# 2 KB pages for all buffers but the activations, one split for each product, and a new order of products in a Strassen short-convolution kernel

## The chip, the cores and the metric

The kernel runs on one core of one Trainium2 chip. The metric is the device time of one execution in microseconds. Before the change it is 792.23 us, the median of 3 runs (791.69 to 792.39).

## The reference

One layer of a gated short-convolution block, on one sequence of 1024 frames with 1024 channels, all in float32. `w_in` is 1024 x 8192 (four branches of 2048), `conv_w` is 3 x 2048, `w_out` is 2048 x 1024.

```python
u = rms_norm(h, pre_norm)
z, bg, cg, v = split(u @ w_in, 4)
y = bg * causal_dwconv(cg * v, conv_w) * silu(z)
m = y @ w_out
out = h + rms_norm(m, post_norm)
```

## The kernel before

**Arithmetic.** TensorE multiplies in `fp32r`. Every operand is split into a high part (the rounded value, ScalarE, line 140) and a low part (value minus high, VectorE, line 141), and a product is three matmuls: low x high, high x low, high x high (lines 189 to 191). On top of this stands one level of Strassen's method in the Winograd form: a product of 2 x 2 blocks takes seven block products, named a, b, c, e, d, f and g, instead of eight.

**Pairs.** The 2048 channels of a branch are taken in 16 chunks of 128. A chunk makes two *pairs* p: the even one multiplies the columns of cg and v, the odd one those of z and bg. A pair is seven products; a product is 4 x 3 = 12 matmuls of 512 columns. Pair 0 is done as plain products and pair 1 among the preparation; the loop of line 646 runs over p = 2 to 31 and takes the products of each in `ORDER`, "abcedfg".

**Weights of a pair.** `fetch` loads two row blocks of `w_in` into one tile `raw` of 8 KB per partition (two DMAs of 512 KB, line 121), one or two pairs ahead. `add_s` forms four sums of blocks on GpSimd (POOL): e, then c, d, f (lines 133 to 137), in one tile `sum` with a single buffer. `split_w` splits two blocks with one ScalarE and one VectorE instruction of 128 x 1024 (part 0: a and b; 1: c and e; 2: d and f) and g alone with 128 x 512 (part 3). The parts of pair q = p + 1 are issued after the products b, e, f and g of pair p, so the weights are split five to seven products before use.

**Results of a pair.** Four products pile up in the PSUM bank x (a, c, d, g), two in v (e, f), and b has its own, y. `snap` (line 197) copies x after a and after c, and v after e, to SBUF; the next product into that bank waits for the copy. VectorE adds b, d and f to these copies (lines 213, 218, 223). After g of an even pair VectorE multiplies into `gpad` (line 236) and `conv` (lines 573 to 580) runs: a scaled copy on ScalarE (line 575), then two VectorE instructions of 128 x 1024 (line 577) into a tile `cv`, which has two buffers. The odd pair multiplies the other factors into `cv` and stores it (`y_done`).

**Side work.** `fetch_t` and `add_t` form the block combinations of `w_out` for one chunk (four subtractions, on VectorE for even p, lines 275 to 278), for p = 4, 6, ... 16 and 17; `add_y` forms those of y (line 257, or lines 261 to 263). Both store their result in DRAM.

**Output stage.** After pair 31 the seven products of the output projection run over 28 *units* of four 128 x 512 blocks, loaded by `fetch_unit` (one DMA of 1 MB each) and split by `split_unit`; `combine` and `finish` normalise, add the residual and store.

**Order.** The schedule is manual: each engine runs its instructions in the order in which the code issues them, and so does the queue of SP, which issues nearly all DMAs. An instruction that waits holds back all that is behind it on its engine.

**Buffers.** `raw` has three tiles of 8 KB per partition and `sum` one; the split weights `wp` three of 8 KB and two of 4 KB; `snp` five of 2 KB; `tmp` holds `gpad`, `cv` and one more of 2 KB; `up` has seven of 16 KB for the activations, which are split once; PSUM has eight banks.

## Time and profile before

| | |
|---|---|
| median of the runs shown | 792.23 us |
| the profiled execution: its own time | 791.43 us |
| its span, first to last instruction | 789.6 us |
| TensorE (PE) busy | 781.3 us, 3494 matmuls |
| VectorE (DVE) busy | 532.2 us, 578 instructions |
| ScalarE (ACT) busy | 309.3 us, 425 instructions |
| GpSimd (POOL) busy | 293.4 us, 197 instructions |
| HBM read and written | 84.4 and 29.4 MB |

In the profile's rows L141 is line 141 of the kernel, and `w<-sum,w` means that tile w is written from tiles sum and w. A row of the timeline has the start and the duration in us, the engine, the line, the operation, the tiles and shapes, the count, and in brackets the idle time before it with what ended that. Times are from the start of the span. PEld is TensorE's weight load, SPq the DMA queue of SP. Two names are used below: T is the start of the first matmul behind product g of an even pair, and a *lo* (*hi*) is the VectorE (ScalarE) instruction of a split.

### The profile page before, as it was taken

The numbers are of one execution on the slowest core, as the hardware profiler recorded it, in microseconds if no ns is written. First come the engines' busy times: TensorE is split into PE (matmuls) and PEld (weight loads), VectorE is DVE, ScalarE is ACT, GpSimd is POOL, SyncE is SP. The second block draws the span as 40 slices with busy tenths as digits, with TensorE's granted clock in tenths as the row PEclk, the third lists the DMA queues.
The fourth block names the chain that finished last, engine by engine and source line by source line (L and its number), as shares of the span: only waits on it lengthen the run. The fifth ranks groups of instructions, "written<-read, shape, count | busy, mean of one in ns | idle before, by whom it ended". The sixth has DMA issues, their size and how long they took to land.

```text
span 789.6 us, 9038 instructions
## 1 busy us (share of the span) xinstructions
PE 781.3 (99%) x3494; PEld 647.9 (82%) x3494; DVE 532.2 (67%) x578; ACT 309.3 (39%) x425; POOL 293.4 (37%) x197
## 2 busy tenths in 40 slices
PE   9999999999999999999999999999999999999996
PEld 8888888888888888888888888888888888888885
DVE  6799676767676767586666666666666857633766
ACT  8555423333333333332333232333332636544441
POOL 2618644444444444456444444434443100000020
PEclk9999999999999999999999999999999999999999
DMA  9130370707061625246232414141505569455237
GB/s 319 56 99 8 94 238 16 253 1 253 26 228 43 212 67 187 93 164 207 95 127 75 147 54 148 53 148 52 180 22 198 215 233 415 180 198 213 107 110 263
DMA packets 94282, 114.38 MB, mean 145 GB/s; under 512 B 2920, under 2 KB 68512, under 8 KB 92192
## 3 DMA queue, kind: packets, MB, share of 16 engines
q1 hardware_dynamic: 94224, 113.81, 42.4%
q8 instruction: 27, 0.44, 0.2%
q14 instruction: 15, 0.12, 0.0%
q10 hardware_dynamic: 16, 0.00, 0.0%
HBM read 84.44 MB, written 29.36 MB: 144 GB/s over the span
## 4 chain that ended last, share of the span: by engine, by line
PE 98%; DVE 0%; DMA 0%; ACT 0%; issue 0%; DVEq 0%
PE px L189 14%; PE px L190 14%; PE px L191 14%; PE pv L189 7%; PE pv L191 7%; PE pv L190 7%; PE po_x L708 4%; PE po_x L709 4%; PE po_x L707 4%; PE py L189 4%; PE py L191 4%; PE py L190 4%; PE po_v L708 2%; PE po_v L709 2%; PE po_v L707 2%; PE pp L388 1%
## 5 line engine op out<-in xcount | busy, mean ns | idle before, releaser
L141 DVE TENSOR_TENSOR w<-sum,w 128x1024 fp32r<-128x1024 f32 x62 | 93.7, 1511 | 77.3 <-ACT w L140 77.3
L141 DVE TENSOR_TENSOR w<-raw,w 128x1024 fp32r<-128x1024 f32 (+1 forms) x62 | 98.3, 1587 | 5.2 <-ACT w L140 5.2
L140 ACT CAST w<-sum 128x1024 fp32r<-128x1024 f32 x62 | 65.0, 1049 | 63.1 <-issue 54.5
L577 DVE SCALAR_TENSOR_TENSOR cv<-gpad,cw,cv 128x1024 f32<-128x1024 f32 x32 | 63.7, 1989 | 20.2 <-ACT cv L575 19.6
L140 ACT CAST w<-raw 128x1024 fp32r<-128x1024 f32 (+1 forms) x62 | 51.5, 833 | 59.9 <-PE py L191 59.9
L228 POOL TENSOR_TENSOR gpad<-snc,sne 128x512 f32<-128x512 f32 x15 | 20.4, 1360 | 138.9 <-DVE snc L223 138.9
L136 POOL TENSOR_TENSOR sum<-raw 128x512 f32<-128x512 f32 x31 | 61.0, 1969 | 0.0
L220 POOL TENSOR_TENSOR sne<-sne,cv 128x512 f32<-128x512 f32 x15 | 20.4, 1363 | 100.6 <-DVE sne L218 85.2
L223 DVE TENSOR_TENSOR snc<-pv,snc 128x512 f32<-128x512 f32 x30 | 20.7, 691 | 54.3 <-PE pv L191 54.3
L747 POOL TENSOR_TENSOR acc<-acc,xr 128x512 f32<-128x512 f32 x4 | 6.9, 1719 | 133.1 <-DVE acc L746 133.1
L137 POOL TENSOR_TENSOR sum<-raw,sum 128x512 f32<-128x512 f32 x31 | 54.6, 1763 | 0.0
L133 POOL TENSOR_TENSOR sum<-raw 128x512 f32<-128x512 f32 x31 | 41.5, 1337 | 31.4 <-DVE w L141 31.4
L189 PE MATMUL py<-u_b,w 128*128 128x512 f32 x124 | 48.4, 391 | 0.0
L189 PE MATMUL px<-u_a,w 128*128 128x512 f32 x124 | 48.3, 390 | 0.0
L191 PE MATMUL py<-u_b,w 128*128 128x512 f32 x124 | 48.2, 389 | 0.0
L190 PE MATMUL py<-u_b,w 128*128 128x512 f32 x124 | 48.2, 389 | 0.0
L191 PE MATMUL px<-u_a,w 128*128 128x512 f32 x124 | 48.2, 389 | 0.0
L190 PE MATMUL px<-u_a,w 128*128 128x512 f32 x124 | 48.2, 389 | 0.0
L189 PE MATMUL px<-u_c,w 128*128 128x512 f32 x124 | 48.2, 389 | 0.0
L190 PE MATMUL px<-u_c,w 128*128 128x512 f32 x124 | 48.2, 389 | 0.0
L191 PE MATMUL px<-u_c,w 128*128 128x512 f32 x124 | 48.2, 389 | 0.0
L189 PE MATMUL pv<-u_e,w 128*128 128x512 f32 x124 | 48.2, 389 | 0.0
(259 smaller groups left out, 2073.7 us busy)
## 6 DMA issues: line engine op xcount, KB each, us to landing
raw<-in_sc_w_in SPq DMA_DIRECT2D x64, 512.0 KB, 5.4
y_d<-cv SPq DMA_DIRECT2D x16, 512.0 KB, 3.2
t<-in_sc_w_out SPq DMA_DIRECT2D x8, 1024.0 KB, 5.9
t_d<-t SPq DMA_DIRECT2D x8, 1024.0 KB, 4.3
s_d<-s SPq DMA_DIRECT2D x8, 768.0 KB, 3.6
s<-y_d SPq DMA_DIRECT2D x8, 512.0 KB, 4.5
xr<-in_x SPq DMA_DIRECT2D x8, 512.0 KB, 4.5
out<-acc SPq DMA_DIRECT2D x12, 256.0 KB, 2.5
```

Of the source, the lines that this page charges most:

```text
L133: nc.gpsimd.tensor_add(s[:, 1], a21, a22)
L136: nc.gpsimd.tensor_sub(s[:, 2], a11, a21)
L137: nc.gpsimd.tensor_sub(s[:, 3], a12, s[:, 0])
L140: nc.scalar.copy(hi, src)
L141: nc.vector.tensor_sub(lo, src, hi.bitcast(F32))
L189: nc.tensor.matmul(ps, lo, UH[i][:, k], start=first and k == 0, stop=False, skip_group_check=True)
L190: nc.tensor.matmul(ps, hi, UL[i][:, k], start=False, stop=False, skip_group_check=True)
L191: nc.tensor.matmul(ps, hi, UH[i][:, k], start=False, stop=last, skip_group_check=True)
L577: nc.vector.scalar_tensor_tensor(cv, gpad[:, j : j + L], tap(c, j), cv, op0=ALU.mult, op1=ALU.add)
L707: nc.tensor.matmul(ps, lo, u[:, 0, k], start=first, stop=False, skip_group_check=True)
L708: nc.tensor.matmul(ps, hi, u[:, 1, k], start=False, stop=False, skip_group_check=True)
L709: nc.tensor.matmul(ps, hi, u[:, 0, k], start=False, stop=last, skip_group_check=True)
```

## The change

All tiles but the activations, `gpad`, `cv` and a few of the ends become pages of 128 x 2 KB in one pool of 36. `fetch` fills four pages with four DMAs of 256 KB; each sum is a page (d overwrites a block of `raw`); each product's weights are two pages, split by one hi and one lo of 128 x 512. `cv` has one buffer. Products run in the order of `slots`: c e d f of pair p, then a and b of pair p + 1, then g of p. After product n, `prepare` issues the splits of all products whose nominal start (2.72 us each) lies less than 7 us behind that of product n + 1: of product n + 3, that is. The functions whose names begin with `deep` run only for chunks from `DEEP` on, and with `DEEP = 16` there are none; they are left out here.

```diff
+PAGES = 36
+DEEP = 16
+LEAD = 7.0
...
-    wp = ctx.enter_context(tc.tile_pool(name="wp", bufs=3))
-    raw = ctx.enter_context(tc.tile_pool(name="raw", bufs=3))
+    pages = ctx.enter_context(tc.tile_pool(name="pages", bufs=PAGES))
...
+    def page(name, dtype=F32, shape=(HB,)):
+        return pages.tile([P, *shape], dtype, tag="pg", name=name, bufs=PAGES)
...
     def fetch(p, rows=(0, 1)):
...
-            nc.sync.dma_start(raws[p][:, n], wiv[:, :, c0 : c0 + P])
+            for k in (0, 1):
+                if (p, n, k) not in raws:
+                    raws[p, n, k] = page(f"raw_{p}_{n}{k}", shape=(KH, P))
+                nc.sync.dma_start(raws[p, n, k], wiv[:, k * KH : (k + 1) * KH, c0 : c0 + P])
...
+    def add_s(p, kinds):
...
+        for i in kinds:
+            if i == "d":
+                t = block(p, 1, 0)
+                nc.gpsimd.tensor_sub(t, block(p, 0, 0), t)
+            else:
+                t = page(f"s{i}_{p}")
+                if i == "e":
+                    nc.gpsimd.tensor_add(t, block(p, 1, 0), block(p, 1, 1))
+                elif i == "c":
+                    nc.gpsimd.tensor_sub(t, sums[p, "e"], block(p, 0, 0))
+                else:
+                    nc.gpsimd.tensor_sub(t, block(p, 0, 1), sums[p, "c"])
+            sums[p, i] = t
...
+    def split_w(p, kinds):
...
+        for i in kinds:
+            hi, lo = (page(f"w{i}{h}_{p}", F32R) for h in "hl")
+            split(block(p, *BLOCK[i]) if i in BLOCK else sums[p, i], hi, lo)
+            wt[p, i] = hi, lo
...
     def add_t(j, eng):
...
+        for n in range(4):
+            nc.sync.dma_start(t_d[:, n, j], t[n])
...
     def square(t):
-        out = flat(raws[0][:, 0]) if t == 0 else junk
+        out = block(0, 0, 0).bitcast(BF16) if t == 0 else junk
...
-            fetch(2)
         rs = pre_rstd([t])
...
     low_plain(0, 1)
+    fetch(2)
...
-    split_w(2, 0)
+    split_w(2, "ab")
...
-    add_s(2, 0)
-    add_s(2, 1)
+    add_s(2, "ecdf")
     fetch(3)
     def conv(c):
-        cv = tmp.tile([P, L], F32, tag="cv", name=f"cv_{c}", bufs=2)
+        cv = tmp.tile([P, L], F32, tag="cv", name=f"cv_{c}")
...
-            split_w(2, 1)
+            split_w(2, "c")
             conv(0)
...
+    slots = [("a", 2), ("b", 2)]
+    for p in range(2, len(PAIRS)):
+        q = p + 1
...
+        for i in "cedf":
+            slots.append((i, p))
...
+        if q <= END:
+            slots.append(("a", q))
...
+                slots.append(("b", q))
+        slots.append(("g", p))
...
+    def prepare(n):
+        while ready[0] < len(slots) and at[ready[0]] < at[n + 1] + LEAD:
+            i, p = slots[ready[0]]
...
+            elif (p, i) not in wt:
+                split_w(p, i)
+            ready[0] += 1
...
+    for n, (i, p) in enumerate(slots):
...
+        product(p, i)
+        prepare(n)
+        after(p, i)
+        q, prev = p + 1, p // 2 - 1
...
+        if i == "c":
+            if p % 2 and p // 2 < DEEP:
+                nc.scalar.activation(sn[p, "a"], sn[p, "a"], AF.Silu)
+            if p in TODO:
+                fetch_t(TODO[p])
+            if p % 2 == 0 and p > 2:
+                fetch_s(prev)
...
+        elif i == "e":
+            add_s(q, "ec")
+        elif i == "d":
+            if p + 2 <= END:
+                fetch(p + 2)
+            add_s(q, "d")
+            if p % 2 == 0 and p > 2:
+                add_y(prev)
+        elif i == "f":
+            add_s(q, "f")
+            if p == 2:
+                add_y(0)
...
+        elif i == "g":
+            if p in TODO:
+                add_t(TODO[p], nc.gpsimd if p % 2 else nc.vector)
...
+        if p == END - 1 and i in "cd":
+            fetch_unit()
+        if p == END and i in "acdg":
+            split_unit()
+            fetch_unit()
```

The output stage follows: a unit is four pages with four DMAs of 256 KB and four splits of 128 x 512 (two of 128 x 1024 before), four units instead of five are split ahead of it, and the residual, the post-norm row and three of the result blocks become pages of 128 x 512 with a DMA each.

## The prediction

> **What bounds the kernel now.** I read the totals first, then the stretches, then TensorE's own waits.

> ```profile
> span 789.6 us, 9038 instructions
> ...
> PE 781.3 (99%) x3494; PEld 647.9 (82%) x3494; DVE 532.2 (67%) x578; ACT 309.3 (39%) x425; POOL 293.4 (37%) x197
> ```
> ```profile
> core 0: us, PE busy (x) PEld busy (x) DVE busy (x) ACT busy (x) POOL busy (x), PEclk, DMA share, GB/s
> 0.00:13.00 13.00, 11.27 (x78) 10.75 (x79) 5.67 (x28) 9.63 (x18) 2.31 (x8) 1.00 0.89 290
> 13.00:60.00 47.00, 46.95 (x228) 38.70 (x228) 42.78 (x57) 28.19 (x41) 19.14 (x16) 1.00 0.39 122
> 60.00:100.00 40.00, 40.00 (x179) 33.10 (x178) 32.18 (x29) 18.77 (x24) 29.61 (x17) 1.00 0.16 47
> 100.00:614.00 514.00, 514.00 (x2269) 425.64 (x2268) 343.02 (x312) 173.94 (x229) 231.79 (x152) 1.00 0.39 126
> 614.00:650.00 36.00, 36.00 (x161) 29.80 (x160) 26.60 (x25) 17.01 (x21) 3.65 (x2) 1.00 0.65 229
> 650.00:783.00 133.00, 133.00 (x588) 109.87 (x586) 79.24 (x122) 60.80 (x92) 6.88 (x4) 1.00 0.58 217
> 783.00:789.60 6.60, 0.10 (x1) 0.00 (x0) 2.74 (x8) 0.98 (x3) 0.00 (x0) 0.75 0.42 163
> ```

> From 13 to 783 us TensorE has no gap: 770 us of stream, 0.05 us idle, at full clock. One matmul takes 514.00 / 2269 = 0.2265 us, a product of twelve 2.72 us. The change issues the same 3494 matmuls, so nothing it does between 13 and 783 us can shorten the run; it can only open gaps. What could be gained lies in the first 13 us and the last 6.6 us. The question is therefore whether the other engines, given smaller pieces and less lead, still deliver each product's weights in time.

> **Head and tail.** In the head, high_plain and low_plain become two instructions each. What hides this is ScalarE's wait for the transposes:

> ```profile
> 12.06 2.42 ACT L354 ACTIVATE u_a<-pk,gcol 128x512 fp32r<-128x512 f32 x4 [0.39 <-PE pk L342]
> ...
> 12.80 0.50 PE L386 MATMUL pp<-u_a,wn 128*128 128x512 f32 x1
> ...
> 118.91 0.61 ACT L140 CAST w<-raw 128x512 fp32r<-128x512 f32 x1
> ...
> 119.45 0.59 ACT L197 COPY sna<-px 128x512 f32<-128x512 f32 x1
> ```

> A hi of 512 occupies ScalarE for 0.54 us (118.91 to 119.45), two for 1.08, against about 0.95 for one of 1024: +0.13 us inside 0.39 us of waiting. Without that cover it would cost 0.13 us once. The square's bf16 output goes to scratch nobody reads; I take nothing for it. fetch(2) keeps its place on SP's queue, behind the conv_w load. Loads carry the same bytes in twice the issues, and DMA is 89% busy here, so bytes and not issues set the landing. In the tail the last row's chain has the same instructions: 0.

> **The loop: SP, pages, ScalarE.** Raw loads become 128 issues of 256 KB:

> ```profile
> raw<-in_sc_w_in SPq DMA_DIRECT2D x64, 512.0 KB, 5.4
> ```

> fetch(p + 2) moves from behind product a to behind d of pair p, past `fetch_t` and `fetch_s` on SP. None of these waits for TensorE, so SP reaches it as soon as the y store behind the odd g is out (1.9 us after that g), needs some 4 us for eight issues and 5.4 to land: 11.3 us after g. POOL, which has nothing to wait for either once it is past the multiplication behind f, reaches the first reader, sum e, at about 10.9 + 0.9 + 1.25 + 0.6 + 1.25 = 14.9: 3.6 us to spare, 0. The four t_d stores now stand behind g and hold SP until add_t is done, 7.4 us after it; the raw load queued behind them then lands at 7.4 + 1.8 + 5.4 = 14.6, just ahead of its sum e, and if it is late the sums move behind an odd g, where VectorE has room: 0. Pages: at the worst point, behind d of an even pair, I count raw blocks 4 + 4 + 1, sums 3, four products' weights 8, copies 4, w_out 4, y sums 3: 31 of 36, so no wait: 0. The single `cv` is freed by `add_y` behind d, while the next `conv` comes behind g, four products later: 0. Behind each copy that a product waits for lies one whole product (2.72 us against 0.59): 0, but at the start.

> **VectorE and POOL take turns.** This sets the price of a late lo:

> ```profile
> 571.75 1.29 POOL L228 TENSOR_TENSOR gpad<-snc,sne 128x512 f32<-128x512 f32 x1 [9.93 <-DVE snc L223]
> ...
> 572.11 2.02 DVE L141 TENSOR_TENSOR w<-sum,w 128x1024 fp32r<-128x1024 f32 x1 [0.44 <-ACT w L140]
> ...
> 574.05 0.68 DVE L236 TENSOR_TENSOR gpad<-px,sna 128x512 f32<-128x512 f32 x1
> ...
> 576.00 4.19 DVE L577 SCALAR_TENSOR_TENSOR cv<-gpad,cw,cv 128x1024 f32<-128x1024 f32 x2 [1.28 <-ACT cv L575]
> ...
> 576.83 2.28 POOL L136 TENSOR_TENSOR sum<-raw 128x512 f32<-128x512 f32 x1
> ...
> 580.12 1.77 DVE L141 TENSOR_TENSOR w<-raw,w 128x512 fp32r<-128x512 f32 x1
> ...
> 614.07 2.61 DVE L577 SCALAR_TENSOR_TENSOR cv<-gpad,cw,cv 128x1024 f32<-128x1024 f32 x2 [1.27 <-ACT cv L575]
> ...
> 616.60 0.69 DVE L141 TENSOR_TENSOR w<-raw,w 128x512 fp32r<-128x512 f32 x1
> ```

> The lo at 572.11 ends at 574.13, which is 1.09 us behind the end of POOL's 571.75 + 1.29 = 573.04: it waited out POOL's instruction. With POOL busy the two conv instructions take 4.19 us, alone 2.61; a 512 lo 1.77, alone 0.69. VectorE work from PSUM (574.05) is untouched. So each POOL instruction that falls between two SBUF instructions of VectorE costs it one turn of about 1.25 us.

> [...] What it makes of this change: seven lo instead of four a pair are seven places where a turn can be lost; that is the third case below.

> **The tight place: behind g of an even pair.** Before, the splits were five to seven products ahead; now three, and VectorE works behind g of an even pair in this order: multiply into gpad, conv, for p = 4 to 16 add_t (moved there from behind b), then the lo of f of the odd pair, which must be ready three products (8.16 us) after T.

> ```profile
> 102.94 0.39 PE L189 MATMUL px<-u_c,w 128*128 128x512 f32 x1
> ...
> 103.21 0.69 DVE L213 TENSOR_TENSOR sna<-py,sna 128x512 f32<-128x512 f32 x1 [0.73 <-PE py L191]
> ...
> 107.11 0.69 DVE L275 TENSOR_TENSOR t<-t 128x512 f32<-128x512 f32 x1 [1.15 <-DMA t<-in_sc_w_out]
> ...
> 109.77 0.68 DVE L257 TENSOR_TENSOR s<-cv 128x512 f32<-128x512 f32 x1
> ...
> 117.09 0.68 DVE L236 TENSOR_TENSOR gpad<-px,sna 128x512 f32<-128x512 f32 x1
> ...
> 117.85 1.16 ACT L575 ACTIVATE cv<-gpad,cw 128x1024 f32<-128x1024 f32 x1 [2.74 <-DVE gpad L236]
> ...
> 119.04 4.20 DVE L577 SCALAR_TENSOR_TENSOR cv<-gpad,cw,cv 128x1024 f32<-128x1024 f32 x2 [1.27 <-ACT cv L575]
> ```

> VectorE can start 0.27 us after T (102.94 to 103.21). Gpad to scaled copy 0.76 (117.09 to 117.85), copy to conv 1.19 (to 119.04): T + 2.22. Conv alone 2.53 (614.07 to 616.60): T + 4.75. Four subtractions 2.66 (107.11 to 109.77): T + 7.41. The lo: T + 8.10. TensorE takes it up about 0.05 us later and its first matmul behind a wait is 0.11 longer (0.50 at 12.80 against 0.39): T + 8.26. Late by 0.10 us, seven times: **0.7 us**. Bounds: 0 if the weight load hides (T + 8.15), and one turn of POOL, 1.25 us, in each of the seven windows, 8.8 more. I take 0.7 since POOL should be through: behind f it has a multiplication and three sums, 5.0 us, with three lo's between, 1.8, from 0.9 us after f: 7.7, against 8.16 when T comes and 10.4 when conv starts. Odd pairs and even ones without add_t have 2.66 us to spare: 0. t lands long before g, so its DMA doesn't hold VectorE.

> **The start of the loop.** `prepare` comes behind conv(0), and the copy of x after a(2) behind that on ScalarE.

> ```profile
> 57.29 1.22 DVE L141 TENSOR_TENSOR w<-raw,w 128x1024 fp32r<-128x1024 f32 x1
> ...
> 58.42 1.28 DVE L396 TENSOR_TENSOR sp<-pp,sp 128x512 f32<-128x512 f32 x2
> ...
> 60.82 0.76 DVE L588 TENSOR_TENSOR gpad<-sp,sp 128x512 f32<-128x512 f32 x1
> ...
> 63.07 0.56 ACT L197 COPY sna<-px 128x512 f32<-128x512 f32 x1
> ...
> 59.74 1.29 POOL L134 TENSOR_TENSOR sum<-sum,raw 128x512 f32<-128x512 f32 x1
> ...
> 60.99 1.74 POOL L136 TENSOR_TENSOR sum<-raw 128x512 f32<-128x512 f32 x1
> ...
> 64.86 0.39 PE L189 MATMUL px<-u_c,w 128*128 128x512 f32 x1
> ```

> Taking turns (lo 0.60, like each of the four instructions from 58.42 to 60.82; POOL 1.25, from 59.74 to 60.99): lo a to 57.89, sum e to 59.14, lo b to 59.74, then POOL c and d to 62.24; VectorE's four PSUM instructions (58.42 to 60.82, 2.40) end at 62.14, L588 waits for d and ends at 62.84; sum f to 64.09, lo c to 64.69. ScalarE: scaled copy 62.90 to 64.06, hi e 0.54, copy of x 0.59: 65.19. That copy stood at 63.07; product c began at 64.86 and now must wait to 65.25: 0.4. Conv from 64.69 ends at 67.22, lo e at 67.91, in use at 68.07 against 67.98: 0.1. Together **0.5 us**; bounds 0 (the turns fall well) and one more turn, 1.75.

> [...]

> **Sum.** 0.5 + 0.7 = 1.2 us: span 790.8, and 792.6 against the profiled execution's own 791.43 (1.8 lie outside the span). The median of the runs shown is 0.8 above that execution; on it, 792.23 + 1.2 = 793.4 us.

> **Rivals.**
> - *Nothing shows, 792.2 us.* The gaps are sums of margins near a tenth; the weight load may hide and the turns fall well. For it: 40.00 of 40.00 us busy even in the crowded stretch from 60 to 100. Chance 0.24.
> - *Forecast, 793.4.* 0.42.
> - *Slower: POOL's sums run into the window behind g.* The sums of the next pair need raw pages; if POOL is held for those, or for a free page, so that it ends over 2.7 us later than I reckon (10.4 - 7.7), one sum falls between the conv instructions and the lo of f is a turn late: 7 x 1.35 + 0.5 = 10 us, 802; a window hit in part of the chunks gives 796 to 800. For it: VectorE has no slack there. Against: the 3.6 us to spare of the loads come on top. 0.30 with its partial forms.
> - *Faster: the finer raw pages or bf16 scratch let the first product start earlier.* Against: the 0.39 us wait is for TensorE's transposes, not for weights; at most that, 791.8, and more only if the head's DMAs reorder. 0.04.

> **How the numbers follow.** 0.2% (1.6 us) is about what a measurement of this kernel can tell from no change. Slower by more holds the third case and a quarter to a third of the forecast's spread, 0.30 + 0.14 = 0.44; faster 0.03; the rest, 0.53, is within. The range from 791.7 to 799 leaves out the full form of the third case and the deeper part of the last. The forecast's own range is 792.2 to 795.

> **What would show it.** Right: TensorE stays gapless from 100 us but for about 0.1 us before f of pairs 5, 7, ... 17, ended by VectorE's L141 low part; about 0.4 us before c of pair 2, ended by ScalarE's copy; conv near 2.6 us instead of 4.2. Wrong: conv still at 4 us behind g (POOL late), waits of ScalarE or VectorE for a page's DMA, gaps in the output stage, or the first weight matmul away from 12.8 us.

## The result, and the profile after

793.47 us, the median of 17 runs (792.82 to 793.96), against 792.03 us for the kernel before on the same chip (17 runs, 791.48 to 792.50): 1.44 us slower, ratio 1.0018, 95% interval 1.001 to 1.0025.

The totals of the changed kernel's page and its stretches. In the second fence the columns are the stretch, its length, the busy time and instruction count of each engine, the granted clock, the DMA share and GB/s.

```profile
span 791.8 us, 10032 instructions
...
PE 783.6 (99%) x3494; PEld 648.5 (82%) x3494; DVE 507.9 (64%) x729; ACT 319.4 (40%) x576; POOL 279.3 (35%) x197
```
```profile
core 0: us, PE busy (x) PEld busy (x) DVE busy (x) ACT busy (x) POOL busy (x), PEclk, DMA share, GB/s
...
60.00:100.00 40.00, 39.95 (x176) 32.74 (x175) 32.23 (x36) 18.42 (x31) 23.49 (x16) 1.00 0.24 73
100.00:614.00 514.00, 514.00 (x2266) 424.51 (x2265) 312.35 (x393) 175.80 (x308) 224.54 (x153) 1.00 0.39 125
...
785.00:791.80 6.80, 0.00 (x0) 0.00 (x0) 3.62 (x10) 0.95 (x3) 0.00 (x0) 0.75 0.55 210
```

VectorE has 24 us less to do than before (507.9 against 532.2) with 151 more instructions, and none of it is worth anything: TensorE is the bound, as before. The long stretch even reads 514.00 of 514.00 busy, as if there were no gap. That is a trap of this view. A matmul's row is 0.39 us long but the next starts 0.2266 us later, so rows overlap and a gap of a tenth disappears in the overlap. Small gaps are seen only in the starts, row by row. The timeline of the changed kernel, at the start of the loop and behind product g of pair 8 (T = 199.37, where c of pair 9 starts):

```profile
63.47 1.16 ACT L581 ACTIVATE cv<-gpad,cw 128x1024 f32<-128x1024 f32 x1 [1.21 <-DVE gpad L594]
...
64.53 0.61 ACT L154 CAST weh<-se 128x512 fp32r<-128x512 f32 x1
...
65.03 0.58 ACT L196 COPY sna<-px 128x512 f32<-128x512 f32 x1
...
65.22 0.39 PE L190 MATMUL py<-u_b,wbh 128*128 128x512 f32 x1
...
65.67 0.50 PE L188 MATMUL px<-u_c,wcl 128*128 128x512 f32 x1
66.00 0.39 PE L189 MATMUL px<-u_c,wch 128*128 128x512 f32 x1
...
196.42 1.62 POOL L148 TENSOR_TENSOR sc<-se,raw 128x512 f32<-128x512 f32 x1
...
199.37 0.39 PE L188 MATMUL px<-u_c,wcl 128*128 128x512 f32 x1
199.57 0.69 DVE L236 TENSOR_TENSOR gpad<-px,sna 128x512 f32<-128x512 f32 x1 [0.98 <-PE px L190]
...
201.53 2.61 DVE L583 SCALAR_TENSOR_TENSOR cv<-gpad,cw,cv 128x1024 f32<-128x1024 f32 x2 [1.27 <-ACT cv L581]
...
204.06 0.69 DVE L281 TENSOR_TENSOR t<-t,t 128x512 f32<-128x512 f32 x1
...
206.71 0.68 DVE L155 TENSOR_TENSOR wfl<-sf,wfh 128x512 fp32r<-128x512 f32 x1
...
207.08 0.19 PEld L190 LDWEIGHTS px<-u_d,wdh 128*128 128x128 f32 x1
...
207.30 0.39 PE L190 MATMUL px<-u_d,wdh 128*128 128x512 f32 x1
...
207.51 0.19 PEld L188 LDWEIGHTS pv<-u_f,wfl 128*128 128x128 f32 x1 [0.25 <-issue]
...
207.54 0.47 PE L188 MATMUL pv<-u_f,wfl 128*128 128x512 f32 x1
207.85 0.39 PE L189 MATMUL pv<-u_f,wfh 128*128 128x512 f32 x1
```

Product c of pair 2 starts 65.67 - 65.22 = 0.45 us after the matmul ahead of it, 0.22 too late, right when ScalarE's copy of x (65.03 + 0.58) ends, and its first matmul takes 0.33 to the next, 0.10 too long: 0.32 us. Product f of pair 9 starts 0.24 after the matmul ahead of it, with a first step of 0.31: 0.10 us; the same is found ahead of f of pairs 5, 7, 11, 13, 15 and 17 and nowhere else behind 40 us.

One table holds what the profiles of all runs say. The stream is the time from the start of the first weight matmul to that of the last matmul; the tail runs from there to the end of the span. The last column is the median against that of the kernel before on the same chip.

| kernel | first weight matmul at | stream | tail | median against before |
|---|---|---|---|---|
| before, three profiles | 12.80, 13.10, 13.41 | 769.91, 769.95, 769.97 | 6.94, 6.93, 6.93 | |
| after | 13.35 | 771.19 | 7.30 | +1.44 |
| differences moved | 13.39 | 770.27 | 7.10 | +0.58 |
| copy ahead of splits | 13.53 | 771.11 | 7.46 | +1.71 |
| longer lead | 12.96 | 770.88 | 7.09 | +0.73 |
| residual earlier | 13.11 | 771.24 | 7.10 | +1.44 |
| differences moved, e early | 12.97 | 769.97 | 7.23 | +0.12 |
| all three | 13.84 | 769.91 | 7.11 | -0.07 |
| GpSimd ahead of its sums | 13.78 | 801.00 | 7.10 | +29.49 |
| GpSimd behind its sums | 12.97 | 778.38 | 7.11 | +8.53 |

The stream of the kernel before repeats within 0.06 us, so it is the measure by which the experiments below are read; the change made it 1.28 us longer than in the first profile. The tail is 0.36 us longer in this profile of the changed kernel and 0.16 to 0.18 in most of the others with pages.

### The profile page after: what moved, and what is told of

Read it like the earlier page. It is cut to its first block, busy times and chain, and to the rows that moved or that the text cites. A ratio compares the mean times of both kernels' runs of the same rounds, so it can differ in the third digit from the quotient of the medians.

```text
span 791.8 us, 10032 instructions
## 1 busy us (share of the span) xinstructions
PE 783.6 (99%) x3494; PEld 648.5 (82%) x3494; DVE 507.9 (64%) x729; ACT 319.4 (40%) x576; POOL 279.3 (35%) x197
## 4 chain that ended last, share of the span: by engine, by line
PE 90%; DVE 5%; DMA 2%; ACT 1%; issue 1%; POOL 0%; SPq 0%; DVEq 0%; ACTq 0%
PE px L188 14%; PE px L189 14%; PE px L190 14%; PE pv L188 7%; PE pv L189 7%; PE pv L190 7%; PE py L188 3%; PE py L189 3%; PE py L190 3%; PE po_x L859 3%; PE po_x L857 3%; PE po_x L858 3%; PE po_v L859 2%; PE po_v L857 2%; PE po_v L858 2%; DMA xr<-in_x 1%
## 5 line engine op out<-in xcount | busy, mean ns | idle before, releaser
L146 POOL TENSOR_TENSOR se<-raw,raw 128x512 f32<-128x512 f32 x31 | 48.9, 1579 | 3.5 <-PE px L190 2.6
L188 PE MATMUL pv<-u_f,wfl 128*128 128x512 f32 x124 | 48.8, 393 | 0.0
L188 PE MATMUL py<-u_b,wbl 128*128 128x512 f32 x124 | 48.4, 391 | 0.0
L188 PE MATMUL px<-u_c,wcl 128*128 128x512 f32 x124 | 48.3, 390 | 0.1
L188 PE MATMUL px<-u_a,wal 128*128 128x512 f32 x124 | 48.3, 390 | 0.0
L190 PE MATMUL pv<-u_f,wfh 128*128 128x512 f32 x124 | 48.3, 390 | 0.0
L189 PE MATMUL pv<-u_f,wfh 128*128 128x512 f32 x124 | 48.3, 390 | 0.0
L189 PE MATMUL pv<-u_e,weh 128*128 128x512 f32 x124 | 48.3, 389 | 0.0
L190 PE MATMUL px<-u_c,wch 128*128 128x512 f32 x124 | 48.3, 389 | 0.0
L188 PE MATMUL pv<-u_e,wel 128*128 128x512 f32 x124 | 48.3, 389 | 0.0
L190 PE MATMUL py<-u_b,wbh 128*128 128x512 f32 x124 | 48.3, 389 | 0.0
L189 PE MATMUL px<-u_c,wch 128*128 128x512 f32 x124 | 48.2, 389 | 0.0
L189 PE MATMUL py<-u_b,wbh 128*128 128x512 f32 x124 | 48.2, 389 | 0.0
## 6 DMA issues: line engine op xcount, KB each, us to landing
y_d<-cv SPq DMA_DIRECT2D x16, 512.0 KB, 3.0
xa<-in_x SPq DMA_DIRECT2D x4, 512.0 KB, 5.2
```

The source lines that it names most:

```text
L146: nc.gpsimd.tensor_add(t, block(p, 1, 0), block(p, 1, 1))
L188: nc.tensor.matmul(ps, lo, UH[i][:, k], start=first and k == 0, stop=False, skip_group_check=True)
L189: nc.tensor.matmul(ps, hi, UL[i][:, k], start=False, stop=False, skip_group_check=True)
L190: nc.tensor.matmul(ps, hi, UH[i][:, k], start=False, stop=last, skip_group_check=True)
```

## The experiments

**The four differences moved** (e1). In even pairs `add_t` goes from behind g, ahead of the low part of f, to behind product e of the next odd pair.

```diff
         elif i == "e":
...
+            if p % 2 and p - 1 in TODO:
+                add_t(TODO[p - 1], nc.vector)
...
-            if p in TODO:
-                add_t(TODO[p], nc.gpsimd if p % 2 else nc.vector)
+            if p in TODO and p % 2:
+                add_t(TODO[p], nc.gpsimd)
```

> add_t of even pairs moved from behind g to behind product e of the next (odd) pair, all else as in the changed kernel. Theory (VectorE's queue behind g is what makes the low part of f late): the low part of f is then done at about T + 5.4 instead of T + 8.0, the seven gaps of 0.10 us before f of pairs 5 to 17 go, and the time falls by 0.7 us, from 793.47 to about 792.8. Rival (the shorter lead of the splits as such, or the 256 KB loads of w_out): the seven gaps stay or move to another product and the time stays within 0.2 us of the changed kernel.

792.51 us (11 runs) against 791.93, ratio 1.0007 (0.9998 to 1.0016). The low part of f is done at T + 5.37, the seven gaps ahead of f are gone and the stream is 771.19 - 770.27 = 0.92 us shorter; the gap ahead of c of pair 2 stays. The four differences in that place are the cause of the seven gaps.

**The copy of x ahead of the splits** (e2). At the first slot of the loop alone, `after` runs before `prepare`, so that ScalarE copies x before it makes the high parts.

```diff
-        prepare(n)
-        after(p, i)
+        if n == 0:
+            after(p, i)
+            prepare(n)
+        else:
+            prepare(n)
+            after(p, i)
```

> Only at the first slot (a of pair 2) the copy of x comes ahead of the split of e instead of behind it. Theory (product c of pair 2 waits for ScalarE's copy, which stands behind one high part too many): the copy ends 0.5 us earlier, the gap before c of pair 2 shrinks from 0.22 + 0.10 us to at most 0.1, time down 0.3 us. Rival (c waits for its own low part, which ends at 65.13 in the changed kernel, or for POOL's sums): the gap stays above 0.2 us.

793.64 us (11 runs) against 791.93, ratio 1.0022 (1.0013 to 1.003). The gain of 0.3 did not come. The timeline of this run says why:

```profile
67.72 0.69 DVE L155 TENSOR_TENSOR wel<-se,weh 128x512 fp32r<-128x512 f32 x1
...
68.12 0.39 PE L190 MATMUL px<-u_c,wch 128*128 128x512 f32 x1
...
68.46 0.50 PE L188 MATMUL pv<-u_e,wel 128*128 128x512 f32 x1
...
68.79 0.40 PE L189 MATMUL pv<-u_e,weh 128*128 128x512 f32 x1
```

c starts in time, and the next product stalls instead: the low part of e (67.72 + 0.69) stands behind conv(0) on VectorE, and e has to wait 0.11 us and loses another 0.10 with its first step. In the changed kernel c's own delay hides this. The stream is 0.08 us shorter, not 0.32, and the median does not show even that (+1.71 against +1.44).

**A longer lead** (e3). `LEAD` is 9.8 instead of 7.0: each product is split one product earlier, so the low part of f is made ahead of conv.

> LEAD 9.8 instead of 7.0: every split is issued one product earlier (four ahead). Theory: the low part of f then stands ahead of the conv on VectorE, and behind g comes that of the next a, due one product later, so the seven gaps before f go (0.7 us less); at the start ScalarE has one more high part (0.54 us) ahead of the copy of x, so the gap before c of pair 2 grows from 0.32 to about 0.85 us. Together about 0.2 us less than the changed kernel. Rival (add_t at this place costs TensorE whatever the lead): the gaps stay, now before a.

792.71 us (11 runs) against 791.98, ratio 1.0011 (1.0002 to 1.002). There is no gap ahead of any f, although the four differences are back behind g: what f waits for is its low part, and the differences matter only because they stand ahead of it. The start pays, for one more high part stands ahead of the copy of x on ScalarE:

```profile
64.18 0.60 ACT L154 CAST weh<-se 128x512 fp32r<-128x512 f32 x1
...
64.69 0.62 ACT L154 CAST wdh<-raw 128x512 fp32r<-128x512 f32 x1
...
64.81 0.39 PE L190 MATMUL py<-u_b,wbh 128*128 128x512 f32 x1
...
65.21 0.58 ACT L196 COPY sna<-px 128x512 f32<-128x512 f32 x1
...
65.84 0.50 PE L188 MATMUL px<-u_c,wcl 128*128 128x512 f32 x1 [0.64 <-ACT sna L196]
```

The gap ahead of c is now 65.84 - 64.81 - 0.23 = 0.80 us, and here the profile names its releaser, ScalarE's copy. One high part more holds ScalarE for 0.52 us there (64.69 to 65.21), and the gap is 0.80 - 0.22 = 0.58 longer. The stream is 0.32 us shorter, where 0.2 was expected; the medians differ by 0.7, more than the stream explains.

**The residual four rows ahead** (e4). `load_res` is called for row t + 4 instead of t + 2.

```diff
-        if t + 2 < NT:
-            load_res(t + 2)
+        if t + 4 < NT:
+            load_res(t + 4)
...
-            load_res(0)
-            load_res(1)
+            for t in range(TH):
+                load_res(t)
```

> The residual rows are loaded four rows ahead instead of two. Theory (the two half-row loads of row 6 land late, VectorE waits 1.35 us for them, and the last row starts behind that): VectorE has no wait for xr any more, and the stretch from the last matmul's start to the end falls from 7.26 us (784.54 to 791.8) to about 6.9, as in the kernel before (782.71 to 789.6); time down 0.2 to 0.3 us. Rival (the last row's own chain from the copy to the store sets the end): the stretch stays at 7.2 us.

793.37 us (11 runs) against 791.93, ratio 1.0019 (1.001 to 1.0028). The waits for `xr` are gone from the tail, but it is 7.10 us long and not 6.9, and the median does not tell it from the changed kernel (+1.44 both). Four profiles that load the residual as the changed kernel does have a tail of 7.09 to 7.11 too, so no gain of this edit is shown. The tail is taken up below.

**The kernel before, twice again** (e0, e0b), for the scatter of its head and tail.

> The kernel before once more, for the head: the first matmul with weights starts at 12.80 us in its profile and at 13.35 in that of the changed kernel. If this 0.55 us belongs to the change, this run shows 12.8 again and all variants of the changed kernel about 13.3; if it is how the first loads of x happen to land, the starts scatter over both values in both.

> The kernel before a third time, for the head. In its two profiles the third load of x has landed when ScalarE wants it (square at 7.13 and 7.18 us) and the first weight matmul comes 8.72 us behind the first square; in three of four profiles with pages the third square comes at 8.0 to 8.2 and the matmul 9.1 to 9.4 us behind the first. If that belongs to the pages, it is 8.72 here again, and 9.1 or more in most of the other runs of this batch.

791.77 and 792.09 us. Both stand in the first row of the table: stream and tail repeat within 0.06, while the first weight matmul moves by 0.6 us, because the loads of x land at different times: the square of its third block starts between 7.13 and 8.07 us. With pages it starts between 7.15 and 8.50.

**Differences moved, and e of pair 2 split early** (e7). The edit of e1, and the splits of both c and e of pair 2 issued ahead of conv(0).

```diff
-            split_w(2, "c")
+            split_w(2, "ce")
```

> add_t moved as in the run with the moved add_t, and at the start c and e of pair 2 are split together ahead of the first conv, as in the kernel before. Theory (these two places are all that the change costs TensorE behind 13 us): the matmul stream is gapless from 60 us to the end as in the kernel before, and the time is that of the kernel before up to the landing of the loads at both ends, 792.0 to 792.5. Rival (pages, smaller splits and the new order cost something of their own): gaps elsewhere, time above 792.8.

792.10 us (11 runs) against 791.98, ratio 1.0002 (0.9993 to 1.001). No gap over 0.02 us behind 40 us, and the stream is 769.97, as before the change. So of the 1.28 us the differences make 0.92 and the start 0.30, and no more than the 0.06 of the scatter is left over for pages, DMA issues, the single `cv` or the smaller pieces.

**All three corrections** (e9): e7 and e4 together.

> All three corrections in the changed kernel: the four differences of even pairs moved behind product e of the next odd pair, the low part of e of pair 2 made ahead of the first conv, and the residual loaded four rows ahead. Theory: the same 792.1 as the run with the first two, less the 0.2 of the tail: 791.9, no difference from the kernel before (ratio 0.999 to 1.001), since the pages by themselves open nothing that bounds the kernel; no gap of TensorE over 0.02 us behind 40 us and the last row 1.15 us behind the last matmul. Rival (pages free a wait that the gaps hid): 791.5 or less, ratio under 0.9995. The head's load of x scatters by up to 0.9 us between profiles and may hide 0.2 us in one profile, not in the median.

791.89 us (11 runs) against 791.96, ratio 1.0001 (0.9992 to 1.001). There is no gap over 0.02 us behind 40 us, and the last row starts 1.15 us behind the last matmul. Its stretches:

```profile
60.00:100.00 40.00, 40.00 (x178) 33.13 (x177) 32.14 (x36) 18.37 (x31) 23.91 (x17) 1.00 0.24 73
100.00:614.00 514.00, 514.00 (x2270) 425.74 (x2269) 318.53 (x394) 176.81 (x310) 223.97 (x153) 1.00 0.39 125
```

With every wait removed that the trace shows in the loop, the pages are worth what the tiles before were. No version beats the kernel before by more than can be measured.

**GpSimd in the window behind g** (e5). The rival that was slower needed sums of GpSimd in that window, which the changed kernel does not have there. Two additions on the gate page, into a page that nobody reads, are put behind the multiplication into `gpad` in the seven even pairs that have `add_t`.

```diff
     def start_conv(c):
         nc.vector.tensor_mul(gpad[:, TAPS - 1 : TAPS - 1 + HB], banks[2 * c, "x"], sn[2 * c, "a"])
+        if 2 * c in TODO:
+            extra = page(f"extra_{c}")
+            for half in (0, 1):
+                nc.gpsimd.tensor_add(extra, gpad[:, 2 : 2 + HB], gpad[:, 2 + HB :])
         conv(c)
```

> Price of one turn in the window: behind g of each even pair that has add_t, POOL does two extra additions of 128 x 512 on gpad into a page that nobody reads; the first falls under ScalarE's scaled copy, the second between that and the first conv instruction. Theory (VectorE and POOL exclude each other for a whole instruction, and VectorE has no slack here): each of the seven gaps before f grows by one turn, from 0.10 to about 1.35 us, and the time by 8.8 us, to 802. Rival (they share, or VectorE's own backlog has slack): gaps under 0.5 us, time under 797.

821.47 us (4 runs) against 791.98, ratio 1.0371 (1.0333 to 1.041): 28 us more than the changed kernel, where some 9 were expected. Timeline of this run behind g of pair 8 (T about 207.3), and one stretch of it in the columns shown above:

```profile
208.38 3.57 POOL L240 TENSOR_TENSOR extra<-gpad 128x512 f32<-128x512 f32 x2 [5.31 <-DVE gpad L236]
...
209.51 3.53 DVE L587 SCALAR_TENSOR_TENSOR cv<-gpad,cw,cv 128x1024 f32<-128x1024 f32 x2 [1.27 <-ACT cv L585]
...
211.93 2.27 POOL L146 TENSOR_TENSOR se<-raw,raw 128x512 f32<-128x512 f32 x1
...
212.97 1.78 DVE L285 TENSOR_TENSOR t<-t,t 128x512 f32<-128x512 f32 x1
...
214.78 1.66 DVE L286 TENSOR_TENSOR t<-t,t 128x512 f32<-128x512 f32 x1
...
218.52 0.76 PE L188 MATMUL pv<-u_f,wfl 128*128 128x512 f32 x1 [2.85 <-DVE wfl L155]
219.08 0.63 PE L189 MATMUL pv<-u_f,wfh 128*128 128x512 f32 x1
219.50 0.63 PE L190 MATMUL pv<-u_f,wfh 128*128 128x512 f32 x1
```
```profile
218.60:221.50 2.90, 2.90 (x7) 2.32 (x8) 2.17 (x4) 0.00 (x0) 1.25 (x1) 0.51 1.02 332
```

Two things were not in the expectation. First, the additions stood 5.31 us at the head of GpSimd's queue, waiting for `gpad`, and held back the sums `se` and `sc` behind them. In the changed kernel these run ahead of T (196.42 + 1.62 = 198.04). So four GpSimd instructions, not two, fell into the window, and three VectorE instructions paid a turn: conv 3.53 for 2.61, two differences 1.78 and 1.66 for 0.69. That is 0.92 + 1.09 + 0.97 = 2.98 us, and all seven gaps ahead of f are 3.0 us, 21 together. Second, in six of the seven windows seven or eight matmuls then run 0.43 us apart instead of 0.2266, at half the granted clock, for some 3 us: 1.5 us lost each time, 9 together. (The last row above reads 0.51 because it reaches 0.08 us past the half-clock stretch.) 21 + 9 is the 30 by which stream and span of this profile grew (it is of an execution of 823.66 us; the four executions lie between 818.62 and 826.22).

**The same additions behind the sums** (e8), to part the two: the additions are issued behind `add_s(q, "ec")` of the odd pair, so that `se` and `sc` run ahead of T again.

```diff
             add_s(q, "ec")
+            if p % 2 and p - 1 in TODO:
+                extra = page(f"extra_{p}")
+                for half in (0, 1):
+                    nc.gpsimd.tensor_add(extra, gpad[:, 2 : 2 + HB], gpad[:, 2 + HB :])
```

> The same two additions of GpSimd on the gate page as in the run before, in seven odd pairs, but issued behind the next pair's sums se and sc, so that these still run ahead of T as in the changed kernel and only the two additions (3.57 us in the run before) stand in the window. Theory (in the run before the additions also drew se and sc into the window: 7.45 us of GpSimd there made VectorE's chain 3.0 us longer, 0.40 per us of GpSimd): here 3.57 x 0.40 = 1.4 us on top of the 0.1 that the low part of f is late already, seven gaps of about 1.5 us ahead of product f, and 793.4 + 7 x 1.4 = 803 us, about the 802 of the rival in the prediction, if the clock is not cut behind a gap as short as this; the conv row of such a pair near 3.5 us and the four VectorE differences behind it near 0.69 again. Rival A (a turn of the two engines is simply dearer than the rows say): the gaps stay near 3 us and the time near 821. Rival B (the clock, and not the wait, made most of the 28 us): gaps of 1.4 but matmuls at 0.43 start to start behind each for some 3 us, 803 + 7 x 1.4 = 813.

800.49 us (4 runs) against 791.96, ratio 1.011 (1.0094 to 1.0125): 7.0 us more than the changed kernel, where the theory said 9.6. The window behind g of pair 8 in this run (T = 200.78):

```profile
201.75 2.68 POOL L801 TENSOR_TENSOR extra<-gpad 128x512 f32<-128x512 f32 x2 [2.30 <-DVE gpad L236]
...
203.22 3.61 DVE L583 SCALAR_TENSOR_TENSOR cv<-gpad,cw,cv 128x1024 f32<-128x1024 f32 x2 [1.55 <-ACT cv L581]
...
206.75 0.69 DVE L281 TENSOR_TENSOR t<-t,t 128x512 f32<-128x512 f32 x1
```

Here only conv pays: 3.61 for 2.61. Conv began as the second addition of 1.3 us had just begun, and waited it out (201.75 + 2.68 = 204.43); the differences cost 0.69 again. This window is one of two in which conv also began 0.28 us later than elsewhere, behind ScalarE's scaled copy (1.55 us of waiting for it against 1.27); in the other five it takes 3.52 or 3.53. The gaps ahead of f are 0.93 to 0.94 us in those five and 1.29 and 1.36 in the two, 7.3 together, and no matmul runs at half pace. That VectorE waits out an instruction of GpSimd is what the prediction reads from its row at 572.11, and it fits here: conv is 1.00 us longer, where 204.43 - 203.22 = 1.21 us of the addition were still to run when it began. Rival A (a dearer turn) and rival B (the clock as the main part) both fall; the size expected from 0.40 per us of GpSimd was too large, since what counts, by these two runs, is not GpSimd's busy time but how many instructions of VectorE meet one of GpSimd.

## Why the prediction was right, point by point

- **Bound and sign.** TensorE's stream had nothing to give and could only open gaps: shown. The stream is 1.28 us longer, the sum said 1.2, and the median moved by 1.44; the slowest execution of the kernel before (792.50) is faster than the fastest of the changed one (792.82), so the rival of no change falls. That 793.4 was forecast and 793.47 measured is in part luck: the start cost 0.30 and not 0.5, the seven gaps 0.92 and not 0.7, the end 0.18 and not 0, and the kernel before stood at 792.03 in this comparison and not at 792.23.
- **The tight place.** Forecast 0.10 us ahead of f, seven times. The window ran as worked out, a few hundredths early: conv at T + 2.16 (2.22 forecast), the differences at T + 4.69 (4.75), the low part of f at T + 7.34 (7.41). The gaps are 0.10 us by the rows and 0.92 / 7 = 0.13 by the stream; moving the differences alone takes them away. The sizing of the first step behind a wait, 0.11, taken from a row of the head, is what made the 0.10: the wait itself is 0.01 to 0.02 and the lengthened step 0.07 to 0.08. The way there was not the one in the sum, and that the two ends agree is luck. The low part was done at T + 8.02, not 8.10, which is 0.14 us before f was due; but the weight load followed 0.12 us later (207.39 to 207.51), not 0.05. In the rows without a gap a weight load starts with the matmul ahead of its own (207.08 for the matmul of 207.30), so f's load was due at 207.30, T + 7.93, and by these rows that is the time by which the low part was needed, not T + 8.16; no run moves it alone to test this.
- **The start of the loop.** Forecast 0.4 for c by ScalarE's copy and 0.1 for e by its low part. c lost 0.32 (0.22 of waiting and 0.10 in the step behind it, where the 0.4 was waiting alone), ended by that copy: e3 names it, and there the gap grows with ScalarE's queue. The e term did not add, since c's delay covers it; it comes up when c's is removed (e2). 0.5 was forecast; the rows say 0.32 and the stream 0.30 to 0.36.
- **POOL and the rival.** GpSimd was through 1.3 us ahead of T (198.04), not 0.5 as reckoned (7.7 against 8.16), and 3.5 ahead of conv, so no turn was lost in the seven windows: conv took 2.61 and not 4.2. The rival's mechanism is real and decides when it comes in. Its price, 1.35 a window, was too high for one turn (e8: 7.0 / 7 = 1.0) and far too low where a waiting GpSimd instruction draws the sums behind it into the window (e5: 3.0 each, and the clock on top).
- **SP, pages, `cv`, ScalarE in the loop at 0.** Shown by e7 and e9, which keep all of them: 769.97 and 769.91 us of stream.
- **The head at 0.** The first weight matmul was at 13.35, not at 12.80, but the kernel before has it anywhere from 12.80 to 13.41, so this says nothing of the change. With pages it lies between 12.96 and 13.84, so the rival of an earlier start is not seen either. Scatter of x's landing, in both kernels; why it scatters was not tried.
- **The tail at 0: the term that was missed.** "In the tail the last row's chain has the same instructions" is true and beside the point. The waits around the chain differ. The first five rows are of the changed kernel, the last two of the run with the moved differences (e1):

```profile
784.54 0.39 PE L859 MATMUL po_x<-ou_g,oy_g 128*128 128x512 f32 x1
784.56 0.75 DVE L904 SCALAR_TENSOR_TENSOR gx<-gx,rs_post,xr 128x512 f32<-128x512 f32 x1 [1.35 <-DMA xr<-in_x]
...
785.89 0.68 DVE L902 TENSOR_TENSOR gx<-po_x,gpost 128x512 f32<-128x512 f32 x1
...
788.75 0.33 SPq L874 DMA_DIRECT2D out<-c  x1
```
```profile
783.66 0.39 PE L861 MATMUL po_x<-ou_g,oy_g 128*128 128x512 f32 x1
...
784.81 0.69 DVE L904 TENSOR_TENSOR gx<-po_x,gpost 128x512 f32<-128x512 f32 x1 [0.45 <-ACT jk L868]
```

In the changed kernel's profile the row ahead of the last waits 1.35 us for its residual, so VectorE takes up the last row 785.89 - 784.54 = 1.35 us behind the last matmul; in the kernel before it is 1.15. These 0.20 us belong to that execution and not to the change: of the six other profiles that load the residual in the same way, five have 1.15 (784.81 - 783.66 above) and one 1.29, so neither a cost nor the worth of e4 is shown by them.

What is there in every profile with pages lies behind the last store. It lands 2.0 us after its issue in both kernels; from there to the end of the span it is 0.90 to 0.91 us in the three profiles of the kernel before, 1.08 to 1.09 in eight of the nine with pages, and 1.44 in e2. The traces show where it goes: the program ends with six waits of SP for the semaphores by which DMAs report their landing, one after the other and some 0.06 us each. In the kernel before (182 issues by SP) the last store has the fifth of these, in the changed one (411 issues) the second, so three more waits stand behind its landing. That is some 0.18 us, and with the 1.28 us of the stream it makes about the 1.44 of the median. That the median of e9 is nevertheless not above that of the kernel before is within what 11 runs tell (0.1%).

## What to carry to other kernels

Where one engine streams without a gap, judge a change by the time from the first to the last instruction of that stream: it repeats within 0.06 us here, where the whole time scatters by 1 us, and a busy share cannot show gaps of a tenth. For each piece of work that moves, add up what its engine does between the event that releases it and the use of the piece: such a sum of rows forecast the place of seven gaps of 0.1 us, though its parts were off by as much as the gap. Take as the use of a weight the start of its load, not that of its matmul (by the rows shown first 207.08 against 207.30; no run tests it alone). When a wait is removed, look at once at the next product, which the wait may have covered (c, then e).
